# A sixth Strassen group, tanh gates and a deeper attention pipeline in a hybrid encoder layer

## The chip, the cores and the metric

The kernel runs on one core of one Trainium2 chip. The metric is the device time of one execution, in microseconds, as the median over runs. The engines are named as in the profile: PE (TensorE, the matrix engine; PEld is its loading of weights), DVE (VectorE), ACT (ScalarE), POOL (GpSimd) and SP (SyncE, which here only issues transfers).

## The reference

One encoder layer over 1024 tokens of width 1024, in float32: half a SwiGLU step, a mixer with two attention branches and gates, half a SwiGLU step, and a final norm.

```python
h = x + 0.5 * swiglu(rms_norm(x, ffn1_norm), ...)            # D_FF = 2816
u = rms_norm(h, mix_norm)
qa, ka, va, qb, kb, vb, ga, gb = split(u @ w_in)             # 512 x 4, 128, 128, 1024, 1024 columns
ya = neighbourhood_attention_2d(qa, ka, va, rpb)             # 8 heads of 64, 16 x 64 grid, 8 x 16 windows
yb = windowed_gqa_sink(rope(qb), rope(kb), vb, sink)         # 8 query heads, 2 key heads, |i - j| <= 128
merged = sigmoid(ga) * (ya @ w_branch_a) + sigmoid(gb) * (yb @ w_branch_b)
h = h + merged @ w_out
h = h + 0.5 * swiglu(rms_norm(h, ffn2_norm), ...)
y = rms_norm(h, final_norm)
```

## The kernel before, in words

Every float32 operand is split into a high and a low part (`split`, lines 91 to 94: ACT copies the high part, DVE or another engine subtracts it to get the low part). Every large product is three matmuls per block of 128 x 128 weights and 512 columns: high by high, high by low, low by high (`mm3`, lines 142 to 149). There are eight PSUM banks in two tags of four, "d" and "g" (`bank`).

The large products use Strassen's scheme in Winograd's form: seven products of quarters instead of eight. For the input projection (`products`, `store_z`) the 34 column chunks of 128 are handled in groups of four chunks, two pairs each; one group is 7 products x 2 pairs x 4 blocks x 3 matmuls. The list `groups` holds five groups: all 18 chunks of queries, keys and values and the first two gate chunks (18 and 19). Chunk 18 + dc is gate chunk dc; dc 0 to 7 belong to branch A and 8 to 15 to branch B. The results go through DRAM tensors (`zs_d`, `z_d`, `g_d`) and are read back where needed.

The remaining 14 gate chunks are computed as ordinary products (`gate`: eight steps of six matmuls each, yielded one by one), and these steps are the *filler* of the attention loop. The filler goes on with branch B's output product (`branch_b`: eight chunks of four steps, each followed by the multiplication by the gate) and with the first steps of branch A's (`branch_a`). `nfill` is the number of steps, 14 x 8 + 38 = 150.

The attention loop goes over 64 units, 32 of branch B and then 32 of branch A. A unit is two heads for 128 queries. Its stages are three functions: `scores` (four matmuls into two "d" banks, on DVE the minimum with the bias, `tensor_tensor_reduce` at line 1283, on ACT the exponential, then the reciprocal on DVE and the scaling of one head's row on DVE, line 1290, and of the other on ACT, line 1291); `turn` (transposes on PE into two "d" banks, line 1299, and a split on ACT and DVE into `ws`); and `values` (matmuls into a "g" bank, lines 1313 and 1318, and the unit's `write` of its output, lines 1231 to 1259). In round n of the loop the program runs `scores` of unit n, half of the round's filler, `turn` of unit n - 1, the other half of the filler and `values` of unit n - 2. `rate`, (150 - 44) / 64 = 1.656, is the number of filler steps per round, and three steps are given in advance. What filler is left runs behind the loop. `prep_a` loads the operands of the next pair of branch A's heads on POOL's queue during the loop, lines 1090 and 1092, and transposes its values, line 1104. Instructions are put in order by a scheduler that follows the order of the program and may move ready ones ahead; the waits follow from what each instruction reads and writes.

Branch B's attention output is collected in an `xs` tile and written to `y_d` from POOL's queue once in four units; branch A's in `fa[:, 3072:4096]`, once in four units, with the last pair of heads split into slots 22 and 23 behind the loop. The rows of the softmax lie in `fa` from column 1536 on, in two pairs used in turn. Behind the loop come branch A's output product with its gates (`a_prep`, `combine`), the product with `w_out` (`Down` with a scale of 1.0), and the second SwiGLU.

## Time and profile before

| | us |
|---|---|
| median of 3 runs | 1935.5 |
| lowest and highest run | 1934.52 and 1937.35 |
| profiled execution: span from the first to the last instruction | 1934.8 |
| of it: attention loop, about | 283 (842 to 1125) |
| of it: input projection behind the norm, about | 197 (645 to 842) |

The profile gives the profiled execution's time only as its span; what lies around the span is not in it, and the median of the runs stands 0.7 us above the span. The mean granted clock of PE is 0.998 of full speed.

How to read it: the page gives the busy time of each engine, their shares in 40 slices, and the chain of work that ended last. The groups of instructions give, behind the shapes and the count, the busy time in us and the mean duration of one in ns, and behind the next bar the idle time of the engine just before them and what ended it. The order of time gives start, duration, engine, line and operation. A stretch's row gives the busy time of PE, PEld, DVE, ACT and POOL (with the number of instructions), then the granted clock, the share of the DMA engines and GB/s.

### The profile page before, as it was taken

Reading aid. Unit: us, or ns where it says so; the run is one execution under the profiler, and the core shown is the slowest. Engines: PE = TensorE matmul, PEld = TensorE weight load, DVE = VectorE, ACT = ScalarE, POOL = GpSimd, SP = SyncE. Lnnn points to the kernel's source line nnn. Section 1 sums busy time; section 2 is a strip of 40 time slices with the busy share of each in tenths; the row PEclk is TensorE's granted clock in tenths of the full one; section 3 lists DMA queues with packets and bytes.
Section 4 is the critical chain, followed back from the end, with each engine's and each line's share of the span. In section 5 each row is a group of like instructions: output and inputs, shape, how many; then the busy total and the mean of one; then the engine's idle time right before and its main releaser. Section 6 shows DMA issues by size and latency. Waiting matters only on the chain.

```text
span 1934.8 us, 25499 instructions
## 1 busy us (share of the span) xinstructions
PE 1922.2 (99%) x8956; PEld 1603.1 (83%) x8956; DVE 1437.1 (74%) x2560; ACT 943.6 (49%) x1827; POOL 295.5 (15%) x432
## 2 busy tenths in 40 slices
PE   9999999999999999999999999999999999999998
PEld 7888888888888888888888888878888888888886
DVE  7987765668957788678888857889676566569864
ACT  6532333344446543477877862365333333344453
POOL 0011110013300112211122231010111001005210
PEclk9999999999999999999999999999999999999999
DMA  6344323286234478553458576533423323493341
GB/s 261 100 167 163 129 104 128 86 289 225 88 109 137 159 223 250 185 163 104 116 134 195 184 242 210 169 140 133 147 87 109 126 87 109 140 355 104 112 144 61
DMA packets 151745, 298.70 MB, mean 154 GB/s; under 512 B 14912, under 2 KB 64448, under 8 KB 151616
## 3 DMA queue, kind: packets, MB, share of 16 engines
q1 hardware_dynamic: 123072, 210.53, 33.6%
q0 software_dynamic: 27824, 85.48, 13.3%
q8 instruction: 71, 1.16, 0.3%
q10 hardware_dynamic: 720, 1.05, 0.1%
q14 instruction: 58, 0.48, 0.1%
HBM read 210.50 MB, written 88.27 MB: 154 GB/s over the span
## 4 chain that ended last, share of the span: by engine, by line
PE 88%; issue 7%; POOL 1%; DMA 1%; DVE 1%; ACT 1%; POOLq 0%; SPq 0%; ACTq 0%; DVEq 0%
PE g L149 16%; PE g L147 16%; PE g L145 16%; PE d L149 11%; PE d L147 11%; PE d L145 11%; PE d L1299 2%; PE g L1313 1%; PE g L1318 1%; PE d L1278 1%; PE d L1279 1%; POOL zs_d L889 1%; PE d L138 1%; POOL z_d L891 1%; DMA zr_d<-xs 0%
## 5 line engine op out<-in xcount | busy, mean ns | idle before, releaser
L145 PE MATMUL g<-ar,ws 128*128 128x512 f32 x1128 | 423.1, 395 | 0.6 <-ACT fa L911 0.6
L147 PE MATMUL g<-ar,ws 128*128 128x512 f32 x1128 | 417.2, 390 | 0.9 <-DVE ar L94 0.5
L149 PE MATMUL g<-ar,ws 128*128 128x512 f32 x1128 | 416.1, 390 | 0.2 <-DVE ws L311 0.2
L145 PE MATMUL d<-ar,ws 128*128 128x512 f32 x736 | 282.4, 391 | 0.3 <-ACT ar L810 0.2
L147 PE MATMUL d<-ar,ws 128*128 128x512 f32 x736 | 281.9, 390 | 0.3 <-DVE ar L812 0.3
L149 PE MATMUL d<-ar,ws 128*128 128x512 f32 x736 | 281.6, 390 | 0.5 <-DVE ws L311 0.5
L147 PEld LDWEIGHTS g<-ar,ws 128*128 128x128 f32 x1128 | 211.8, 188 | 46.2 <-DVE ar L94 1.0
L149 PEld LDWEIGHTS g<-ar,ws 128*128 128x128 f32 x1128 | 211.7, 188 | 45.5 <-DVE ws L311 0.7
L145 PEld LDWEIGHTS g<-ar,ws 128*128 128x128 f32 x1128 | 206.4, 188 | 37.8 <-ACT fa L911 1.0
L311 DVE TENSOR_TENSOR ws<-raw,ws 128x512 fp32r<-128x512 f32 x204 | 139.6, 690 | 99.6 <-ACT ws L308 98.8
L308 ACT CAST ws<-raw 128x512 fp32r<-128x512 f32 x204 | 125.1, 620 | 140.6 <-PE g L149 64.4
L145 PEld LDWEIGHTS d<-ar,ws 128*128 128x128 f32 x736 | 138.3, 188 | 29.7 <-ACT ar L810 0.6
L147 PEld LDWEIGHTS d<-ar,ws 128*128 128x128 f32 x736 | 138.4, 188 | 29.6 <-DVE ar L812 0.6
L149 PEld LDWEIGHTS d<-ar,ws 128*128 128x128 f32 x736 | 138.4, 188 | 29.4 <-DVE ws L311 0.7
L93 ACT CAST ws<-raw 128x512 fp32r<-128x512 f32 (+1 forms) x121 | 81.0, 669 | 144.0 <-PE d L149 61.8
L94 DVE TENSOR_TENSOR ws<-raw,ws 128x512 fp32r<-128x512 f32 (+1 forms) x119 | 93.7, 789 | 59.8 <-ACT ws L93 59.3
L414 POOL DMA_DIRECT2D hid<-fx x91 | 49.3, 542 | 431.5 <-DVE fx L474 304.9
L93 ACT CAST ar<-raw 128x512 fp32r<-128x512 f32 (+1 forms) x83 | 56.0, 679 | 94.8 <-PE g L147 55.0
L94 DVE TENSOR_TENSOR ws<-ar,ws 128x512 fp32r<-128x512 f32 x114 | 98.3, 867 | 3.8 <-ACT ws L93 3.7
L145 PE MATMUL g<-ws,ws 128*128 128x512 f32 x232 | 91.0, 392 | 0.0
L149 PE MATMUL g<-ws,ws 128*128 128x512 f32 x232 | 90.5, 390 | 0.0
L147 PE MATMUL g<-ws,ws 128*128 128x512 f32 x232 | 90.3, 389 | 0.0
(313 smaller groups left out, 3607.4 us busy)
## 6 DMA issues: line engine op xcount, KB each, us to landing
raw<-hid SPq DMA_DIRECT2D x70, 512.0 KB
hid<-fx POOLq DMA_DIRECT2D x91, 256.0 KB, 2.4
ar<-in_ffn_w_down_dram SPq DMA_DIRECT2D x32, 512.0 KB
raw<-in_ffn_w_up_dram SPq DMA_DIRECT2D x31, 512.0 KB
raw<-in_ffn_w_gate_dram SPq DMA_DIRECT2D x27, 512.0 KB
raw<-in_w_in_dram SPq DMA_DIRECT2D x27, 512.0 KB
hid<-fa POOLq DMA_DIRECT2D x51, 256.0 KB, 2.7
ar<-zs_d POOLq DMA_DIRECT2D x48, 256.0 KB, 5.3
```

The costliest lines, as they stand in the source:

```text
L93: nc.scalar.copy(dst_hi, src)
L94: (eng or nc.vector).tensor_tensor(dst_lo, src, f32v(dst_hi), op=ALU.subtract)
L138: nc.tensor.transpose(pt[:, c * P:(c + 1) * P], xs[:, (half * 4 + c) * P:(half * 4 + c + 1) * P], ident)
L145: nc.tensor.matmul(b, lhs[0], r[0], start=first, stop=False, **kw)
L147: nc.tensor.matmul(b, lhs[0], r[1], start=False, stop=False, **kw)
L149: nc.tensor.matmul(b, lhs[1], r[0], start=False, stop=last, **kw)
L308: nc.scalar.copy(w[0][:, :512], a)
L311: nc.vector.tensor_tensor(w[0][:, 512:], a, f32v(w[0][:, :512]), op=ALU.subtract)
L414: nc.gpsimd.dma_start(hid[PRODUCTS.index(p), i], src)
L889: nc.gpsimd.dma_start(d[ch * P:(ch + 1) * P, cols], t)
L891: nc.gpsimd.dma_start(z_d[ch * P:(ch + 1) * P, cols], c)
L1299: nc.tensor.transpose(pt[:, i * P:(i + 1) * P], un["pr"][s][:, i * P:(i + 1) * P], ident)
```

## The change

- `groups` gets a sixth group, gate chunks 20 to 23 (dc 2 to 5). Ten gate chunks are left for the filler, and `nfill` becomes 118.
- The gates' sigmoid becomes tanh: sigmoid(x) = (1 + tanh(x / 2)) / 2. ACT computes tanh(x / 2), DVE computes (tanh + 1) times the branch's product in one instruction, and the factor of one half goes into the scale of the product with `w_out`.
- In the loop, `turn` works on unit n - 2 and `values` on unit n - 3. The rows of the softmax get a third pair in `fa`, and the small statistics a third buffer. `rate` becomes (118 - 17) / 67 = 1.507.
- GpSimd takes over the copy of the sink logit (before on DVE), the scaling of the second head's row (before on ACT), and the low parts of the filler's gate weights and of branch B's weights (before on DVE).
- The attention output is added up in one DVE instruction of 64 partitions in place of two, in `hs` tiles, and written to `y_d` from SP's queue in place of POOL's, once in two units; the transfer puts the halves into their rows. The last pair of heads is split within the loop, once in four units.
- Branch B's gates are fetched two chunks ahead, in halves, into `xs` or `hs` tiles, and opened one chunk ahead.

```diff
-    groups = [[(12, 13), (14, 15)], [(16, 17), (0, 1)], [(4, 5), (8, 9)], [(2, 3), (6, 7)], [(10, 11), (18, 19)]]
+    groups = [..., [(10, 11), (18, 19)], [(20, 21), (22, 23)]]
...
+    def fetch_gate(dc):
+        r = xs4() if dc % 3 < 2 else None
+        rb = [hs4() if r is None else r[:, n * 512:(n + 1) * 512] for n in range(2)]
+        for n in range(2):
+            nc.sync.dma_start(rb[n], g_d[D + dc * P:D + (dc + 1) * P, n * 512:(n + 1) * 512])
         return rb
+    def open_gate(rb):
+        for r in rb:
+            nc.scalar.activation(r, r, AF.Tanh, scale=0.5)
...
-        nxt = branch_w(wb[0], 0, nc.vector), gate_b(0)
+        w, rbs = branch_w(wb[0], 0, nc.gpsimd), [fetch_gate(dc) for dc in range(2)]
+        open_gate(rbs[0])
         for dc in range(NC8):
             bs = [bank("dg"[dc % 2]) for _ in range(2)]
-            yield from branch_mm(bs, w, Y_B)
-            if dc + 1 < NC8:
-                nxt = branch_w(wb[0], dc + 1, nc.vector), gate_b(dc + 1)
+            mm = branch_mm(bs, w, Y_B)
+            for c in range(4):
+                drain(mm, 1)
+                yield
+                if c == 0 and dc + 2 < NC8:
+                    rbs.append(fetch_gate(dc + 2))
+                if c == 1 and dc + 1 < NC8:
+                    nxt = branch_w(wb[0], dc + 1, nc.gpsimd)
+                    open_gate(rbs[dc + 1])
+            w = nxt
             for n in range(2):
-                nc.vector.tensor_tensor(merged(dc)[:, sl], bs[n], rb[:, sl], op=ALU.mult)
+                nc.vector.scalar_tensor_tensor(out=merged(dc)[:, sl], in0=rbs[dc][n], scalar=1.0, in1=bs[n],
+                                               op0=ALU.add, op1=ALU.mult)
...
-                yield from gate(dc, {4: lambda: mix.update(gate=load_w(win[0], GA + nxt * P))})
+                yield from gate(dc, {4: lambda: mix.update(gate=load_w(win[0], GA + nxt * P, eng=nc.gpsimd))})
...
-                    for s in range(2):
-                        nc.vector.tensor_tensor(ybox["b"][s * HD:s * HD + HD, c, :], o[:HD, s, :], lo[:, s, :], op=ALU.add)
-                    if c == 3:
-                        nc.gpsimd.dma_start(y_d[:512, j * P:(j + 1) * P].rearrange("(c p) t -> p c t", p=P), ybox["b"])
+                    nc.vector.tensor_tensor(ybox["b"][:, c % 2], o[:HD], lo, op=ALU.add)
+                    if c % 2:
+                        nc.sync.dma_start(y_d[(c - 1) * P:(c + 1) * P, j * P:(j + 1) * P].rearrange("(c s p) t -> p c s t", s=2, p=HD),
+                                          ybox["b"])
...
+                    if hp == 3:
+                        ...
+                        if j % n == n - 1:
+                            cols = slice((j - n + 1) * P, (j + 1) * P)
+                            split(slot(22)[:, cols], slot(23)[:, cols], ybox["a"])
+                        return
...
-            pr = fa[:, 1536 + (2 * (npair[0] % 2) + s) * (384 + ext):][:, :ext + nw]
+            pr = fa[:, 1536 + (2 * (npair[0] % 3) + s) * (384 + ext):][:, :ext + nw]
             if ext:
-                nc.vector.tensor_copy(pr[:, 0:1], un["sink"][s])
+                nc.gpsimd.tensor_copy(pr[:, 0:1], un["sink"][s])
...
-        nc.scalar.activation(un["pr"][1], un["pr"][1], AF.Copy, scale=rc[:, 1:2])
+        nc.gpsimd.tensor_scalar(un["pr"][1], un["pr"][1], rc[:, 1:2], None, op0=ALU.mult)
...
-    rate = (nfill - 44) / 64.0
+    rate = (nfill - 17) / 67.0
...
-        if len(pipe) > 1 and pipe[1] is not None:
-            turn(pipe[1])
+        if len(pipe) > 2 and pipe[2] is not None:
+            turn(pipe[2])
...
-        if len(pipe) > 2 and pipe[2] is not None:
-            values(pipe[2])
-        pipe = pipe[:3]
+        if len(pipe) > 3 and pipe[3] is not None:
+            values(pipe[3])
+        pipe = pipe[:4]
...
-    split(slot(22), slot(23), fa[:, 3072:4096])
...
-    down = Down(4, wo[0], 1.0, place, quarter, ...
+    down = Down(4, wo[0], 0.5, place, quarter, ...
...
-        nc.scalar.activation(r, r, AF.Sigmoid)
+        nc.scalar.activation(r, r, AF.Tanh, scale=0.5)
...
-            nc.vector.tensor_tensor(r[:, sl], bs[n], r[:, sl], op=ALU.mult)
+            nc.vector.scalar_tensor_tensor(out=r[:, sl], in0=r[:, sl], scalar=1.0, in1=bs[n], op0=ALU.add, op1=ALU.mult)
```

More of the change, by code (lines that the diff above doesn't have):

```diff
@@ L872, in trunk_kernel @@
     mix = {}
-    groups = [[(12, 13), (14, 15)], [(16, 17), (0, 1)], [(4, 5), (8, 9)], [(2, 3), (6, 7)], [(10, 11), (18, 19)]]
+    groups = [[(12, 13), (14, 15)], [(16, 17), (0, 1)], [(4, 5), (8, 9)], [(2, 3), (6, 7)], [(10, 11), (18, 19)], [(20, 21), (22, 23)]]
     NG = len(groups)
@@ L1174, in merged, with hs4 @@
         return slot((16, 17, 18, 19, 24, 25, 26, 27)[dc])
-    def gate_b(dc):
-        rb = xs4()
-        nc.sync.dma_start(rb, g_d[D + dc * P:D + (dc + 1) * P, :])
-        nc.scalar.activation(rb, rb, AF.Sigmoid)
-        return rb
+    def hs4():
+        return main.tile([P, 512], F32, tag="hs", bufs=6, name=nm_("hs"))
+    def fetch_gate(dc):
[3 more added lines that the diff above has]
+            nc.sync.dma_start(rb[n], g_d[D + dc * P:D + (dc + 1) * P, n * 512:(n + 1) * 512])
+        return rb
+    def open_gate(rb):
+        for r in rb:
+            nc.scalar.activation(r, r, AF.Tanh, scale=0.5)
     def branch_b():
@@ L1248, in write @@
                 def write(o, j=j, hp=hp):
-                    y = fa[:, 3072:4096]
+                    n = 4 if hp == 3 else 2
+                    if j % n == 0:
+                        ybox["a"] = hs4()
                     lo = mix["lo"][:HD, j % 2]
@@ L1386, in trunk_kernel @@
     loads[0].append(lambda d: d.load_left(2))
-    down = Down(4, wo[0], 1.0, place, quarter, {k: left_d[i] for i, k in enumerate(("P5", "P6", "P3", "P7"))},
+    down = Down(4, wo[0], 0.5, place, quarter, {k: left_d[i] for i, k in enumerate(("P5", "P6", "P3", "P7"))},
                 loads, (8, 10))
```

21 lines of the change are left out of this document (11 added, 10 removed).

## The prediction, made before the change was run

> **What bounds the kernel now.** I read the page first, then the order of time of the matrix engine (PE), then the busy time by stretch, then the groups of instructions inside the attention loop.
>
> ```profile
> span 1934.8 us, 25499 instructions
> PE 1922.2 (99%) x8956; PEld 1603.1 (83%) x8956; DVE 1437.1 (74%) x2560; ACT 943.6 (49%) x1827; POOL 295.5 (15%) x432
> PE 88%; issue 7%; POOL 1%; DMA 1%; DVE 1%; ACT 1%; POOLq 0%; SPq 0%; ACTq 0%; DVEq 0%
> ```
>
> PE is busy 99% and carries 88% of the chain that ended last. But PE ends are modelled, so I look at starts. In the projection (order of time, PE only):
>
> ```profile
> 700.03 0.39 PE L145 MATMUL d<-ar,ws 128*128 128x512 f32 x1
> ...
> 705.93 0.39 PE L149 MATMUL g<-ar,ws 128*128 128x512 f32 x1
> ```
>
> These two stand 26 matmuls apart: 5.90 / 26 = 0.227 us per 128x512 matmul; the 0.39 is latency, not cost. Now the busy time by stretch: projection, attention of branch B, attention of branch A (two rows), and what follows the loop.
>
> ```profile
> 645.00:842.00 197.00, 196.31 (x881) 162.12 (x880) 155.72 (x234) 95.37 (x169) 34.27 (x64) 1.00 0.68 207
> 842.00:982.00 140.00, 139.34 (x817) 121.95 (x815) 114.79 (x392) 110.39 (x280) 21.02 (x36) 1.00 0.46 127
> 982.00:1046.00 64.00, 63.99 (x386) 56.55 (x385) 55.98 (x178) 51.99 (x139) 11.62 (x22) 1.00 0.64 153
> 1046.00:1125.00 79.00, 79.00 (x468) 69.32 (x467) 66.95 (x211) 66.75 (x164) 23.35 (x25) 1.00 0.68 188
> 1125.00:1175.00 50.00, 50.00 (x222) 41.11 (x221) 19.42 (x30) 24.23 (x31) 12.35 (x10) 1.00 0.77 253
> ```
>
> The columns are PE, weight loads, DVE, ACT, POOL, clock, DMA. PE has no gap to win back: 0.7 us idle in the projection, 0.7 us in the loop, clock 1.00. So the time falls only by fewer matmuls and rises by whatever PE comes to wait for. DVE and ACT have their least room in the loop (82 to 87%, and 79 to 84%); POOL stands at 15 to 30%.
>
> **Part 1, the sixth Strassen group.** Gate chunks 2 to 5 leave the filler: 4 chunks x 8 blocks x 6 matmuls = 192. A group adds 7 products x 2 x 4 blocks x 3 = 168. Net 24 fewer, 24 x 0.227 = **-5.4 us**. The group's splits, combinations and POOL stores lie in a stretch with DVE at 155.72 / 197 = 79% and ACT at 48%, beside continuous PE, and stores and next loads follow the pattern of the five groups there: 0 us. If that cover were gone, the nearest price is that stretch's present loss, 0.7 us.
>
> **Part 2, the loop with less filler.** A filler step is 6 matmuls. Before, 150 steps, of which 3 + 67 x 1.656 = 114 run in the loop and 36 behind it; after, 118, of which 3 + 68 x 1.507 = 105.5 in the loop and 12.5 behind. So the loop's cover per unit shrinks, and branch B's output product (32 steps, from step 81, near unit 52) now runs inside. One unit in the PE's order of time:
>
> ```profile
> 903.40 0.34 PE L1278 MATMUL d<-ar,ar 128*128 128x384 f32 x1
> ...
> 904.11 0.63 PE L145 MATMUL g<-ar,ws 128*128 128x512 f32 x2
> ...
> 905.50 0.82 PE L1299 MATMUL d<-ident,fa 128*128 128x128 f32 x6
> 906.07 0.96 PE L1318 MATMUL g<-ws,fx 128*128 128x256 f32 x6
> 906.87 0.34 PE L1278 MATMUL d<-ar,ar 128*128 128x384 f32 x1
> ```
>
> Scores 0.71, one step 1.39, transposes 0.57, values 0.80. The loop took the 140 + 64 + 79 = 283 us of its three rows for 67 rounds, 4.22 each; 0.149 steps less make 4.22 - 0.21 = 4.02 us. What the other engines must fit into that:
>
> ```profile
> L1291 ACT ACTIVATE fa<-fa,rc 128x384 f32<-128x384 f32 x48 | 29.9, 623 | 1.5 <-DVE rc L1289 1.4
> L1282 DVE COPY fa<-nsk 128x1 f32<-128x1 f32 x64 | 8.5, 142 | 4.6 <-DMA z_d<-fa 3.8 <-ACT fa L1286 0.5 <-DMA g_d<-fa 0.3
> L1233 DVE TENSOR_TENSOR xs<-g,s 64x128 f32<-64x128 f32 x64 | 18.0, 281 | 1.0 <-ACT s L1231 0.2
> L1253 DVE TENSOR_TENSOR s<-g,s 64x256 f32<-64x256 f32 x32 | 13.2, 411 | 2.6 <-ACT s L1252 2.3
> L94 DVE TENSOR_TENSOR ws<-raw,ws 128x1024 fp32r<-128x1024 f32 x13 | 15.9, 1224 | 3.4 <-ACT ws L93 3.2
> L94 POOL TENSOR_TENSOR ar<-raw,ar 128x1024 fp32r<-128x1024 f32 x6 | 14.8, 2464 | 22.0 <-ACT ar L93 22.0
> L126 POOL TENSOR_SCALAR st<-st 128x1 f32<-128x1 f32 x20 | 7.6, 379 | 206.3 <-ACT xs L123 206.0
> L1197 DVE TENSOR_TENSOR ar<-d,xs 128x512 f32<-128x512 f32 x8 | 5.2, 686 | 9.6 <-PE d L149 8.3 <-ACT xs L1179 1.1
> L913 DVE SCALAR_TENSOR_TENSOR fa<-d,fa 128x512 f32<-128x512 f32 x16 | 10.9, 686 | 4.0 <-PE d L149 3.8
> L1179 ACT ACTIVATE xs<-xs 128x1024 f32<-128x1024 f32 x8 | 8.5, 1061 | 10.8 <-DMA xs<-g_d 10.7
> ```
>
> DVE per round: branch B 114.79 / 140 x 4.22 = 3.46, less two sink copies 0.28, less the second write 2 x 0.28 - 0.41 = 0.15, less the gate weights' low part 1.22 x 1.656 / 8 = 0.25, gives 2.8 of 4.02 (69%). Branch A 66.95 / 79 x 4.22 = 3.58, less 0.15 and 0.25, 3.2 (79%). Where branch B's product runs beside it, two gate products per four steps add 2 x 0.69 x 1.507 / 4 = 0.52: 3.7 (92%). The scalar-tensor-tensor that replaces L1197 costs what L1197 does: L913 runs it on one input from PSUM and one from SBUF in the same 0.69.
>
> ACT: branch B 3.33 less the scaling 0.62 is 2.7 (67%); branch A 3.57 - 0.62 = 2.95 (73%); beside the product, four steps bring 512 columns of weights and 1024 of tanh, 1.5 x 1.06 = 1.6 (up to 1.9 in halves), for half a gate's split and copies, 1.06: at most 0.3 a round, 3.2 (80%).
>
> POOL: two sink copies (0.38 each at most), the scaling of 384 columns, and a gate's low part 2.46 x 1.507 / 8 = 0.46. The scaling has no row: below lies 0.38 (one column), above the two-input rate, 2.46 x 384 / 1024 = 0.92. It has one input, so I take 0.7, between them. With the 0.6 it has now, 2.5 of 4.02 at most. No engine passes PE: 0 us.
>
> **Part 3, latency.** The softmax of a unit must be done when its transposes come up.
>
> ```profile
> 903.96 0.62 DVE L1283 CUSTOM_DVE_ANT_0 fa<-d,masks,nsk 128x384 f32<-128x384 f32 x1 [0.50 <-PE d L1279]
> 905.11 0.62 DVE L1283 CUSTOM_DVE_ANT_0 fa<-d,masks,nsk 128x384 f32<-128x384 f32 x1
> 906.88 0.62 ACT L1291 ACTIVATE fa<-fa,rc 128x384 f32<-128x384 f32 x1
> 908.96 0.82 PE L1299 MATMUL d<-ident,fa 128*128 128x128 f32 x6
> ```
>
> The unit started at 903.40, was scaled by 907.50, and was transposed from 908.96: 1.46 us spare. One unit deeper gives 4.02 more, the slower scaling takes 0.1 to 0.3 back: about 5.2 us spare. On POOL a queued gate split (2.46) fits into that; so do the sink copies, which can run once the unit three before has been transposed. POOL's queue also holds prep_a's loads, which wait for PE:
>
> ```profile
> POOL ar L1092 <- PE d L1279: 17.2, 3, 12.2
> ```
>
> If scalings stand behind the longest of these, 12.2 - 5.2 = 7 us are lost once (1937); I take 0, since units in hand come ahead of prep_a in the program. On SP, the writes of y now wait for DVE ahead of later weight loads; those are asked for four steps, 4 x 1.39 us, and the units between them, ahead: 0 us.
>
> **Part 4, around the loop.** Behind it PE keeps 12.5 steps, 17 us, where there were 49; the row 1125 to 1175 shows DVE 39% and ACT 48% busy there, half of it branch B's product that has moved into the loop. 0 us. At the loop's start PE waits once, behind DVE (chain, in order of time):
>
> ```profile
> 848.67 1.24 DVE ar L94
> ...
> 849.95 0.50 PE g L147
> ```
>
> Nothing in the change moves that split's place, so I leave its wait; if the freed DVE removes it, about 1.2 us more are won.
>
> **Sum.** 1934.8 is the span; the median of the runs, 1935.5, stands 0.7 above it, and I leave that as it is. 1935.5 - 5.4 = **1930.1 us**, 0.28% less. About 0.2% (3.9 us) is what a measurement of this kernel can tell from no change.
>
> **Rivals.**
>
> *GpSimd and DVE get in each other's way.* In the trace, by source line:
>
> ```profile
> L94 DVE TENSOR_TENSOR ws<-ar,ws x114: 676/685/1793, 421.3 to 1901.7; 128x512 fp32r<-128x512 f32 x114
> L94 DVE TENSOR_TENSOR ws<-d,ws x128: 411/550/560, 852.4 to 1121.2; 128x384 fp32r<-128x384 f32 x96, 128x256 fp32r<-128x256 f32 x32
> L1290 DVE TENSOR_SCALAR fa<-fa,rc x64: 336/420/966, 850.0 to 1117.7; 128x384 f32<-128x384 f32 x48, 128x256 f32<-128x256 f32 x16
> ```
>
> A DVE subtraction with both inputs in SBUF takes up to 1.79 instead of 0.69, the scaling L1290 once 0.97, while the subtraction from PSUM never passes 0.56. The Trainium skill ("SBUF — State Buffer", Who interferes with whom) says why and speaks against this change: DVE and GpSimd share a port pair, taken whole by a DVE instruction with two SBUF inputs or in a two-port mode, or by GpSimd's. The rows agree with it. By that rule each move to GpSimd costs DVE something too. Here the loop's DVE work is mostly from PSUM, and what is exposed is L1290 once a unit: 0.97 - 0.34 = 0.6. In the units beside the product (15 rounds) DVE goes to 3.7 + 0.6 = 4.3 against 4.02, so 0.3 x 15 = 4 us, and with the last head pair's splits (1.1 each, 4 of them) 8 us: 1934 to 1938. Against it: it needs POOL to be ahead at nearly every unit. Chance 0.22.
>
> *PSUM banks, slower than before.* Even chunks of branch B's product take two of the four "d" banks for four steps, 2.65 rounds, and now do so while scores and transposes need them: chunks 0, 2 and 4, about 8 rounds. With two banks left, scores wait for the low parts of the transposes before them and transposes wait for the scores' minimum:
>
> ```profile
> 900.64 0.82 PE L1299 MATMUL d<-ident,fa 128*128 128x128 f32 x6
> ...
> 902.91 0.56 DVE L94 TENSOR_TENSOR ws<-d,ws 128x384 fp32r<-128x384 f32 x1 [0.16 <-ACT ws L93]
> ```
>
> From scores to the second minimum 905.73 - 903.40 = 2.33, from transposes to the last low part 903.47 - 900.64 = 2.83: 5.16 in a row, and 0.5 for the gate products (2 x 0.69 per 2.65 rounds). If nothing overlaps, (5.66 - 4.02) x 8 = 13 us: 1943. If halves overlap as they do now (0.35 at each hand-over) and filler is put between, near 0. It ends slower than before from 5.4 us of waits, and measurably from 9.3 us, 1.2 a round. For it: DVE at 92% exactly there. Against it: prep_a's own transposes (L1104) take "d" banks today, and the waits of PE's weight loads show 0.3 us for them in the whole loop:
>
> ```profile
> PEld d L1104 <- DVE ws L94: 0.3, 1, 0.3
> ```
>
> Chance 0.15, two thirds of it measurably slower.
>
> *The activation table.* Sigmoid cost a load after the loop's exponentials:
>
> ```profile
> 1130.45 1.28 ACT L1179 ACT_TABLE_LOAD   x1
> ```
>
> If tanh needs another table than exp, six chunks x 2 x 1.28 = 15.4 us fall on ACT inside the loop: 3.2 x 16 + 15.4 = 66.6 against 64.3 available, 2 us at least, 15 at most: 1932 to 1945. The Trainium skill ("ScalarE: Activation LUTs", Table sets: the hidden batching unit) lists tanh in the set of exp, by which this costs nothing; the trace before cannot show it. Chance 0.04, nearly all of it slower.
>
> *The count doesn't fall* (the group runs and PE loses as much between its products): 1935.5. Chance 0.02.
>
> **How the numbers follow.** PE stays fed: 0.57, with its own range from 1928.6 (the start's 1.2 and prep_a's 0.3 gone) to 1931.6 (1.5 us of new waits), all of it faster. Same: 0.21 of the port, 0.05 of the banks, 0.02 of the count, 0.28. Slower: 0.01 of the port above its sum, 0.10 of the banks, 0.04 of the table, 0.15. The range runs from 1928.6 less half the runs' spread (1934.52 to 1937.35, so 1.4), 1927.2, to 1939.0, which leaves the slower cases out.
>
> **What would show it.** Right: 24 fewer 128x512 matmuls, starts 0.227 apart, the projection about 38 us longer, rounds near 4.0 us, no PE wait of over 1 us in the loop, one table load for it. Wrong: PE waiting on "d" tiles from unit 52 on (banks), L1290 near 0.97 in the median (port), table loads among the tanh, or transposes waiting on POOL.

## The result, and the profile after

The changed kernel takes 1948.27 us (median of 5 runs, 1945.26 to 1951.55) beside 1936.05 us of the kernel before in the same comparison (5 runs, 1934.52 to 1938.03): a ratio of 1.0062, 95% interval 1.0052 to 1.0073. It is slower by 12 us, where 5.4 us less were predicted. Its profiled execution took 1947.41 us, 2.1 us more than its span. The 0.7 us that the prediction found before the change set a median beside the span of another execution; in the comparisons below, an execution of the kernel before takes 1.7 to 1.9 us more than its own span. A trace shows one execution, and executions of one kernel differ along with the clock that PE was granted: of the changed kernel's five, the one with a span of 1943.3 us has a mean clock of 0.997, the one with 1949.5 us has 0.993.

The page of the changed kernel: span, busy time, PE's granted clock in 40 slices, and the engines' shares of the chain that ended last.

```profile
span 1945.3 us, 25733 instructions
PE 1921.5 (99%) x8932; PEld 1601.0 (82%) x8932; DVE 1429.5 (73%) x2448; ACT 915.4 (47%) x1781; POOL 413.0 (21%) x567
PEclk9999999999999999999999899999999999999999
PE 86%; issue 6%; DMA 2%; ACT 2%; DVE 2%; POOL 2%; SPq 0%; POOLq 0%; ACTq 0%; DVEq 0%
```

24 matmuls are gone, as counted, yet PE's busy time fell by 0.7 us only, and one slice of the clock fell below full: something between 1070 and 1120 us both stopped PE and slowed it. To see which units, I take the first score matmul of units 0, 48 and 63 in PE's order of time, before (L1278) and after (L1303):

```profile
841.93 0.28 PE L1278 MATMUL d<-ar,ar 128*128 128x256 f32 x1
1049.99 0.28 PE L1278 MATMUL d<-ar 128*128 128x256 f32 x1
1114.61 0.28 PE L1278 MATMUL d<-ar,ar 128*128 128x256 f32 x1
```

```profile
879.02 0.28 PE L1303 MATMUL d<-ar,ar 128*128 128x256 f32 x1
1077.17 0.28 PE L1303 MATMUL d<-ar 128*128 128x256 f32 x1
1154.08 0.38 PE L1303 MATMUL d<-ar,ar 128*128 128x256 f32 x1
```

| stretch | before, us | after, us | difference |
| --- | --- | --- | --- |
| up to the loop | 841.9 | 879.0 | +37.1 |
| units 0 to 48 | 208.1 (4.33 a unit) | 198.2 (4.13) | -9.9 |
| units 48 to 63 | 64.6 (4.31) | 76.9 (5.13) | +12.3 |
| from there to the end | 820.2 | 791.2 | -29.0 |

Nearly all of the loss is in the last 15 units, in which branch B's output product now runs. At the 4.13 us of the first 48 they would take 62.0, which is 14.9 less, and the span would end at 1930.4; the forecast, put on the span, is 1929.4. The stretches of the changed kernel by busy time (PE, weight loads, DVE, ACT, POOL, clock, DMA share, GB/s): the projection, the two parts of the loop, and the 24 us in which it happens.

```profile
683.00:879.00 196.00, 195.50 (x866) 161.60 (x865) 138.44 (x203) 82.27 (x142) 33.04 (x63) 1.00 0.64 195
879.00:1077.00 198.00, 195.86 (x1168) 172.98 (x1167) 154.49 (x461) 140.33 (x373) 121.09 (x168) 1.00 0.51 138
1077.00:1154.00 77.00, 67.39 (x370) 57.22 (x369) 61.03 (x172) 53.76 (x135) 44.74 (x37) 0.89 0.67 188
1086.00:1110.00 24.00, 14.94 (x60) 11.95 (x58) 14.56 (x31) 12.18 (x30) 13.76 (x12) 0.64 0.84 220
```

In these 24 us PE is busy for 14.94 at a mean clock of 0.64. A narrower row shows the clock at half of full speed for 17 us:

```profile
1092.50:1109.50 17.00, 10.15 (x32) 8.13 (x33) 8.75 (x23) 8.11 (x18) 7.26 (x6) 0.50 0.69 214
```

PE's order of time shows four waits, each with what ended it:

```profile
1089.66 0.62 PE L149 MATMUL g<-ar,ws 128*128 128x512 f32 x2
1093.63 1.54 PE L1324 MATMUL d<-ident,fa 128*128 128x128 f32 x6 [3.34 <-DVE ws L94]
...
1097.27 1.95 PE L1338 MATMUL g<-ws,fx 128*128 128x256 f32 x6 [0.39 <-DVE ws L94]
1103.44 1.22 PE L145 MATMUL d<-ar,ws 128*128 128x512 f32 x2 [4.22 <-ACT ws L93]
1104.46 1.05 PE L147 MATMUL d<-ar,ws 128*128 128x512 f32 x2
1106.63 1.22 PE L149 MATMUL d<-ar,ws 128*128 128x512 f32 x2 [1.11 <-POOL ws L94]
```

What DVE and POOL did before the first of them:

```profile
1088.57 4.67 DVE L1315 TENSOR_SCALAR fa<-fa,rc 128x384 f32<-128x384 f32 x1
```

```profile
1088.27 4.75 POOL L94 TENSOR_TENSOR ar<-raw,ar 128x1024 fp32r<-128x1024 f32 x2
```

Y_B[0] to Y_B[3] are the four blocks of rows of branch B's attention output, read back for its output product. The row scaling L1315 takes 0.42 us in the median. This one began while POOL subtracted to get the low parts of Y_B[0] and Y_B[1], and ended with them. Everything on DVE stood behind it, the low parts for the transposes first. The last two waits are for branch B's first weights. SP's queue and the chain in order of time show how these come late:

```profile
1095.07 0.58 SPq L1283 DMA_DIRECT2D y_d<-hs  x1
...
1096.86 0.32 SPq L1153 DMA_DIRECT2D raw<-y_d  x1
1097.27 0.93 SPq L1131 DMA_DIRECT2D raw<-in_w_branch_b_dram  x2
```

```profile
1096.86 4.95 DMA raw<-y_d
...
1102.96 2.39 POOL ar L94
1105.34 1.24 POOL ws L94
...
1106.63 1.22 PE d L149 x2
```

A write of y waits for the held DVE; behind it on SP stand the fetch of a gate and that of Y_B[3], and behind them the weights. ACT's cast and POOL's subtraction of Y_B[3] then stand ahead of those of the weights.

### The profile page after: what moved, and what is told of

The parts are those of the page before. It is cut to its first block, busy times and chain, and to the rows that moved or that the text cites. A ratio compares the mean times of both kernels' runs of the same rounds, so it can differ in the third digit from the quotient of the medians.

```text
span 1945.3 us, 25733 instructions
## 1 busy us (share of the span) xinstructions
PE 1921.5 (99%) x8932; PEld 1601.0 (82%) x8932; DVE 1429.5 (73%) x2448; ACT 915.4 (47%) x1781; POOL 413.0 (21%) x567
## 3 DMA queue, kind: packets, MB, share of 16 engines
q10 hardware_dynamic: 720, 1.05, 0.1%
## 4 chain that ended last, share of the span: by engine, by line
PE 86%; issue 6%; DMA 2%; ACT 2%; DVE 2%; POOL 2%; SPq 0%; POOLq 0%; ACTq 0%; DVEq 0%
PE g L149 16%; PE g L145 16%; PE g L147 16%; PE d L149 11%; PE d L145 11%; PE d L147 11%; PE d L1324 2%; PE g L1343 1%; PE d L1303 1%; PE d L1304 1%; PE g L1338 1%; ACT fa L1311 1%; PE d L138 1%; POOL zs_d L889 1%; POOL z_d L891 0%
## 5 line engine op out<-in xcount | busy, mean ns | idle before, releaser
L145 PE MATMUL g<-ar,ws 128*128 128x512 f32 x1096 | 413.6, 394 | 0.5 <-ACT fa L911 0.5
L147 PE MATMUL g<-ar,ws 128*128 128x512 f32 x1096 | 409.5, 390 | 0.4 <-DVE ar L833 0.4
L149 PE MATMUL g<-ar,ws 128*128 128x512 f32 x1096 | 408.8, 390 | 0.2 <-DVE ws L311 0.2
L145 PE MATMUL d<-ar,ws 128*128 128x512 f32 x760 | 293.0, 392 | 4.6 <-ACT ws L93 4.2
L149 PE MATMUL d<-ar,ws 128*128 128x512 f32 x760 | 291.5, 390 | 1.6 <-POOL ws L94 1.1
L147 PE MATMUL d<-ar,ws 128*128 128x512 f32 x760 | 292.2, 390 | 0.3 <-DVE ar L812 0.3
L149 PEld LDWEIGHTS g<-ar,ws 128*128 128x128 f32 x1096 | 205.6, 188 | 44.2 <-DVE ws L311 0.7
L147 PEld LDWEIGHTS g<-ar,ws 128*128 128x128 f32 x1096 | 205.7, 188 | 43.8 <-DVE ar L833 0.8
L145 PEld LDWEIGHTS g<-ar,ws 128*128 128x128 f32 x1096 | 201.2, 188 | 37.3 <-ACT fa L911 0.9
L311 DVE TENSOR_TENSOR ws<-raw,ws 128x512 fp32r<-128x512 f32 x210 | 143.6, 689 | 107.8 <-ACT ws L308 106.9
L145 PEld LDWEIGHTS d<-ar,ws 128*128 128x128 f32 x760 | 142.7, 188 | 34.5 <-ACT ws L93 4.5
L149 PEld LDWEIGHTS d<-ar,ws 128*128 128x128 f32 x760 | 142.7, 188 | 31.8 <-POOL ws L94 1.8
L147 PEld LDWEIGHTS d<-ar,ws 128*128 128x128 f32 x760 | 142.8, 188 | 30.1 <-DVE ar L812 0.9
L93 ACT CAST ws<-raw 128x512 fp32r<-128x512 f32 (+1 forms) x117 | 76.5, 656 | 140.2 <-PE d L149 61.3
L94 DVE TENSOR_TENSOR ws<-raw,ws 128x512 fp32r<-128x512 f32 x98 | 71.5, 730 | 53.2 <-ACT ws L93 53.2
L1316 POOL TENSOR_SCALAR fa<-fa,rc 128x384 f32<-128x384 f32 (+1 forms) x64 | 82.0, 1282 | 61.9 <-DVE rc L1314 40.7
L1311 ACT ACTIVATE fa<-fa,nmx 128x385 f32<-128x385 f32 (+3 forms) x128 | 75.6, 591 | 41.5 <-DVE nmx L1308 38.4
L145 PE MATMUL g<-ws,ws 128*128 128x512 f32 x232 | 91.0, 392 | 0.0
```

The source lines that it names most:

```text
L93: nc.scalar.copy(dst_hi, src)
L94: (eng or nc.vector).tensor_tensor(dst_lo, src, f32v(dst_hi), op=ALU.subtract)
L145: nc.tensor.matmul(b, lhs[0], r[0], start=first, stop=False, **kw)
L147: nc.tensor.matmul(b, lhs[0], r[1], start=False, stop=False, **kw)
L149: nc.tensor.matmul(b, lhs[1], r[0], start=False, stop=last, **kw)
L311: nc.vector.tensor_tensor(w[0][:, 512:], a, f32v(w[0][:, :512]), op=ALU.subtract)
```

## The experiments

Two theories at first: that POOL's long subtractions hold DVE (the expectations call it A, or the port), and B, the weights' load chain at branch B's head. A third, C, is that the loop's filler cover, the PE work that runs while a unit passes the other engines, is too thin. The head of branch B's product is the place where it begins. Later theories are named where they come in: banks (the product takes PSUM banks from the units), load (it brings DVE and ACT too much work) and burst (its head and the preparation of the last head pair fall together). The time of each is its median and the ratio to the kernel before of its own comparison, which lay between 1935.2 and 1936.3 us.

**Y_B's low parts on DVE.**

```diff
-split_y(Y_B[c], c * P, nc.gpsimd) for c in range(2)
+split_y(Y_B[c], c * P, nc.vector) for c in range(2)
-split_y(Y_B[c], c * P, nc.vector if c == 2 else nc.gpsimd)
+split_y(Y_B[c], c * P, nc.vector)
```

> The changed kernel with one thing undone: the low parts of branch B's attention output (four subtractions of 1024 columns, two of them back to back on GpSimd at 1088 us) are made on DVE. Theory A (port): these two subtractions hold what DVE's scaling L1315 needs (4.67 us in place of 0.42), the transposes and the write of y come late, and all that follows is late because of that. A expects L1315 to stay under 1.5 us, the wait of 3.5 us gone, the later waits mostly gone, 1948 to about 1935. Theory B (late start): the wait from 1097 to 1107 is of its own, since branch B's first weights and outputs are fetched behind writes of y on SP's queue and split behind each other on ACT and GpSimd. B expects 3 to 5 us won only: 1943 to 1945, with PE still waiting 6 us or more for the first weights.

Measured: 1942.2 us, 1.0035 (1.0025 to 1.0046): 6.1 of the 12 us are gone by the medians, about half of what theory A forecast. They need not be the hold's alone: POOL's work on Y_B[3] also stood ahead of that on the first weights, and the edit takes both away. The last 15 units, and the same 24 us:

```profile
1077.00:1147.00 70.00, 63.84 (x369) 53.26 (x367) 62.47 (x173) 53.06 (x134) 37.38 (x33) 1.00 0.73 210
1086.00:1110.00 24.00, 20.38 (x118) 16.56 (x117) 20.48 (x55) 18.44 (x46) 10.76 (x12) 1.00 0.86 227
```

No wait is longer than 1.5 us, and the clock stays at 1.00. (The trace is of an execution of 1939.43 us, 2.8 below the median.) But the units still take 4.68 us, not 4.13, and DVE is now busy for 89% of them. Nor is the hold gone. DVE's own subtraction of a row of Y_B, usually 1.21 us, takes 2.69 beside POOL's for the first weights:

```profile
1094.14 2.69 DVE L94 TENSOR_TENSOR ar<-raw,ar 128x1024 fp32r<-128x1024 f32 x1
```

```profile
1094.44 1.30 POOL L94 TENSOR_TENSOR ws<-raw,ws 128x512 fp32r<-128x512 f32 x1
```

**The first head's scaling on ACT.**

```diff
-nc.vector.tensor_scalar_mul(un["pr"][0], un["pr"][0], rc[:, 0:1])
+nc.scalar.activation(un["pr"][0], un["pr"][0], AF.Copy, scale=rc[:, 0:1])
```

> The changed kernel, but the first head's row is scaled on ACT in place of DVE (the second stays on GpSimd), so that DVE has no single-input scaling in SBUF left. Theory A: with nothing on DVE for GpSimd's pair of subtractions to hold, the 3.5 us wait goes and most of the later ones: about 1935 to 1938, if ACT (0.62 more in each unit) keeps up. Theory B: the first weights are as late as before, 1943 to 1945. A third reading, that it is GpSimd's own lateness (its scaling takes 1.39) that PE waits for: no gain, 1948.

Measured: 1948.05, 1.006 (1.0045 to 1.0075), the number of the third reading, GpSimd's own lateness. But the trace shows a hold again: with the scaling gone from DVE, POOL's pair held another instruction:

```profile
1092.80 3.73 DVE L94 TENSOR_TENSOR ar<-raw,ar 128x1024 fp32r<-128x1024 f32 x1
```

```profile
1090.66 4.78 POOL L94 TENSOR_TENSOR ar<-raw,ar 128x1024 fp32r<-128x1024 f32 x2
```

That is DVE's own part of Y_B, usually 1.21 us. The hold belongs to POOL's instructions, not to the scaling. (Against the third reading stands the run further down in which POOL's scaling is left out.)

**A lower filler rate, so that branch B's product begins behind the loop.**

```diff
-rate = (nfill - 17) / 67.0
+rate = (nfill - 44) / 64.0
```

> The changed kernel with one number changed, the filler rate of the kernel before, (118 - 44) / 64 = 1.156 in place of 1.507, so that branch B's output product begins behind the loop and a round has 3.7 us of PE work in place of 4.0. Theories A and B both put the loss where that product begins inside the loop, and expect it gone: 1931 to 1934. If other parts (GpSimd's scaling, the deeper pipeline, less cover for each unit) cost something through the whole loop, it stays above 1938 with waits spread over the units.

Measured: 1944.27, 1.0041 (1.0027 to 1.0055), where A and B expected 1931 to 1934. The long stops are gone: no wait of PE in the last 15 units is longer than 2.0 us, and the clock stays at 1.00. But the loop pays for the thin cover. PE's own need would be 4.13 - (1.507 - 1.156) x 1.39 = 3.64 us a unit; it took 3.71 in the first 48 and 3.87 in the last 15, 7 us in all.

**The writes of y on POOL's queue.**

```diff
-nc.sync.dma_start(y_d[(c - 1) * P:...
+nc.gpsimd.dma_start(y_d[(c - 1) * P:...
-nc.sync.dma_start(y_d[512 + hp * P:...
+nc.gpsimd.dma_start(y_d[512 + hp * P:...
```

> The changed kernel with the writes of y back on GpSimd's queue, so that SP's later fetches stand behind no write that waits for DVE. Theory B: branch B's first weights and outputs are fetched earlier and the wait from 1097 to 1107 shrinks by 5 us or more: 1940 to 1943. Theory A: L1315 is held as long as before and the first wait stays; the fetches behind it come only as much earlier as SP stood still, 0 to 3 us: 1945 to 1949.

Measured: 1946.51, 1.0058 (1.0038 to 1.0079). By the medians SP's order ahead of the weights is worth 1.8 us, which the runs (1945.1 to 1952.5) don't separate from nothing.

**The kernel before, with the group alone.**

```diff
-... [(2, 3), (6, 7)], [(10, 11), (18, 19)]]
+... [(2, 3), (6, 7)], [(10, 11), (18, 19)], [(20, 21), (22, 23)]]
```

> The kernel before with the sixth Strassen group alone: four gate chunks as filler, branch B's product behind the loop as before, so 74 filler steps on 64 units (1.16 a unit, before 1.66); pipeline, sigmoid and engines untouched. Theory C (the loop needs its cover: with fewer filler steps a unit it waits for DVE and ACT, and the prediction's Part 1 is not kept): the 24 matmuls of 0.227 us are saved (5.4 us), and small PE waits of together 5 to 15 us appear all along the loop: 1935 to 1945. Theories A and B (the loss belongs to branch B's product inside the loop alone: GpSimd's long subtractions, and the load chain at its head) expect no new wait: 1935.6 - 5.4 = 1930.

Measured: 1944.21, 1.0047 (1.003 to 1.0064), within theory C's range. Its units take 3.81 and 4.02 us at 1.16 steps, against 3.64 that PE needs: 14 us. The count is saved and more than spent in the loop. Set beside the run of the changed kernel at 1.16 steps (3.71 and 3.87), the deeper pipeline, the tanh and the use of POOL save 7 us in these units. Of that the whole profiled executions show 2.4 (1944.38 and 1942.0) and the medians nothing (1944.21 and 1944.27).

**The changed kernel without the group.**

```diff
-... [(10, 11), (18, 19)], [(20, 21), (22, 23)]]
+... [(10, 11), (18, 19)]]
```

> The changed kernel without the sixth group: five groups, fourteen... that is four chunks more of gate filler, all else as changed (branch B's product still begins inside the loop, with 1.99 filler steps a unit where the changed kernel has 1.51 and the kernel before 1.66). 24 matmuls (5.4 us) come back. Theories A and B (the two waits of 3.6 and 6 to 9 us come with branch B's head, whatever the cover): the same two PE waits at the place where branch B's product begins, 1948.3 + 5.4 = 1953, or 1945 to 1950 if the thicker cover takes up part. Theory C (cover): the waits shrink to almost nothing, 1935 to 1938.

Measured: 1945.91, 1.0055 (1.004 to 1.007). With the fullest cover of all, 4.78 us in the first 48 units, the last 15 take 5.41: 9.5 us lost. PE's waits there:

```profile
PE d L149 <- POOL ws L94: 3.1, 1, 3.1
PE d L1303 <- DVE ar L1212: 2.4, 1, 2.4
```

So what the change does in the loop costs some 10 us by itself, and cover does not hide it. Each half of the change costs by itself nearly what both cost together (9.0 and 10.7 us of 12.2), as if each used up a reserve that the other needs; that reading is not tested further.

**Branch B's first weights fetched and split early.**

```diff
+7: lambda: mix.update(w0=branch_w(wb[0], 0, nc.gpsimd, mix['w0']))
-5: lambda: [fetch_y(c * P) for c in range(2, 4)]
+5: lambda: [mix.update(w0=fetch_branch(raw4()[:, :512], wb[0], 0))] + [fetch_y(...) for c in range(2, 4)]
-w, rbs = branch_w(wb[0], 0, nc.gpsimd), [...]
+w, rbs = mix.pop('w0'), [...]
```

> The changed kernel with branch B's first weights fetched ahead of the rows of Y_B[2] and Y_B[3] and split behind the last gate chunk, ahead of both; nothing else moves. Theory B (PE's second wait, 4.2 + 1.1 us for the weights, is the load chain: a transfer behind Y_B[3]'s on SyncE's queue, and the casts and subtractions in order behind it): the wait for the weights goes, and with it the stretch at half clock; the first wait (3.5 us on the held row scaling) stays: 1939 to 1943. Theory A (GpSimd's long subtractions delay all of it; the chain follows from them): the wait moves to another tile of the same moment (Y_B[2], Y_B[3]) and the time stays at 1946 to 1949.

Measured: 1946.06, 1.0054 (1.0039 to 1.0069). The wait of 4.2 us for the first weights is gone, and the clock is halved for 3.4 us in place of 17. The wait behind the held scaling is still 3.34 us, and new ones of 1.4, 1.3 and 1.1 us stand behind it, the last for the second chunk's weights. By the medians 2.2 us of time went, which the intervals don't separate from nothing; the last 15 units take 4.99 for 5.13. Theory B's chain was there, but what it cost came back in other waits: it isn't the cause by itself.

**Both of these.** (The edits of the first and of the last run.)

> Both edits: the low parts of the rows of Y_B on DVE instead of GpSimd (alone: 1942.2), and branch B's first weights fetched and split ahead of Y_B[2] and Y_B[3]. Theories A and B together (two causes): both waits at branch B's head are gone, and what is left over the kernel before is the small waits of a thinner loop (3 to 5 us) against the 5.4 us that the group saves: 1933 to 1938. If the waits in the loop outside branch B's head count more (theory C): 1939 to 1942, no better than with the first edit alone.

Measured: 1944.73, 1.0045 (1.003 to 1.006), runs from 1941.5 to 1946.2: not better than the first edit alone.

**All of branch B's products in the "g" banks** (with Y_B on DVE, as in the next three).

```diff
-bs = [bank("dg"[dc % 2]) for _ in range(2)]
+bs = [bank("g") for _ in range(2)]
```

> The changed kernel with Y_B's low parts on DVE (alone: 1942.2, 6.6 us above the kernel before) and, new, all of branch B's products in the four "g" banks, so that no chunk takes two of the "d" banks from scores and transposes. Banks theory (the prediction's second rival): PE's waits for "d" tiles from unit 50 on (scores and transposes that wait for DVE's low parts of the transposes before) go: 1937 to 1939, the rounds 48 to 63 go from 4.7 to about 4.3 us. Load theory (branch B's product brings more DVE and ACT work into rounds in which DVE stands at 87%; what comes late isn't made up, and the waits move to whatever tile is next): 1941 to 1944, the waits on other lines.

Measured: 1943.36, 1.0039 (1.0024 to 1.0054). The banks by themselves are not it.

**A rate between.**

```diff
-rate = (nfill - 17) / 67.0
+rate = 1.35
```

> The changed kernel with Y_B's low parts on DVE and the filler rate at 1.35 steps a unit in place of 1.51: branch B's product begins near unit 57 instead of 51, so a third of it is in the loop instead of two thirds, and the rounds ahead of it fall from 4.13 to about 3.9 us. Load theory: less of branch B's work in the loop means less waiting there, and 3.9 us is still above the 3.75 us at which the loop ran with 1.16 steps: 1936 to 1940. Cover theory (any thinner cover loses more than it saves): 1943 to 1946. Banks theory: fewer chunks in the loop's "d" banks, 1939 to 1941.

Measured: 1947.32, 1.0061 (1.0044 to 1.0077), the wrong way for the load theory: 3.96 us in the first 48 units, where PE needs 3.91, and 4.67 in the last 15. It pays for both.

**Branch B's tanh at the gate's copy.**

```diff
-nc.scalar.copy(gt[:, n * 512:(n + 1) * 512], bs[n])
+nc.scalar.activation(gt[:, n * 512:(n + 1) * 512], bs[n], AF.Tanh, scale=0.5)   # dc >= 8
-open_gate(rbs[0])
-open_gate(rbs[dc + 1])
```

> The changed kernel with Y_B's low parts on DVE and the tanh of branch B's gates taken where ACT copies a gate chunk out of PSUM (the copy becomes the tanh), so that the sixteen tanh of 0.64 us at branch B's product, which wait in ACT's order for the gates' transfers, are gone. Load theory: 10 us of ACT's work less in 14 rounds, and ACT's order no longer waits for a transfer; ACT stands at 80% there: 1938 to 1941. Banks theory, and DVE's share of the load theory: no change, 1941 to 1943.

Measured: 1942.25, 1.0033 (1.002 to 1.0046). 10 us of ACT's work gone, and nothing of the time.

**Y_B on DVE, "g" banks and early tanh.**

> Three edits: Y_B's low parts on DVE, branch B's products all in the "g" banks, its gates' tanh taken early. If banks and ACT's load both hold: 1934 to 1938. If only one of them does: as that one alone. If neither does (DVE's load, or the order of all of it): 1941 to 1944.

Measured: 1940.45, 1.0021 (1.0012 to 1.003), the best of all, and still slower than before; the 1.8 us below the first edit alone are not clear of the spread. The last 15 units take 4.50.

**Less work on DVE, and on POOL.** Y_B on DVE, and one scaling of each unit left out:

```diff
-nc.vector.tensor_scalar_mul(un["pr"][0], un["pr"][0], rc[:, 0:1])
```

> The changed kernel with Y_B's low parts on DVE (alone: 1942.2), with the row scaling of the first head of each unit left out (L1315, DVE 0.42 us a unit; the output is not normalised there). Load theory (DVE at 87 to 95% in the rounds beside branch B's product): DVE gets 10% of a round back and PE's waits there fall to a third or less: 1934 to 1937. If GpSimd's slow scaling or the order of the queues is the cause: 1940 to 1943.

```diff
-nc.gpsimd.tensor_scalar(un["pr"][1], un["pr"][1], rc[:, 1:2], None, op0=ALU.mult)
```

> The changed kernel with Y_B's low parts on DVE (alone: 1942.2), with the row scaling of the second head of each unit left out (L1316, GpSimd 1.39 us a unit; the output is not normalised there). If GpSimd's scaling is the cause (its 1.39 us in the softmax's latency, its queue of scalings behind the splits, or the time in which it holds DVE): 1934 to 1937. Load theory of DVE: DVE's work stays, no more than the stretched instructions fall: 1940 to 1943.

Measured: 1941.17, 1.0032 (1.0021 to 1.0042), and 1943.09, 1.0036 (1.0024 to 1.0047). Neither 10% less work on DVE nor a POOL without its scaling moves these units much. What held the first one's head, from the waits of all engines between 1085 and 1130 us:

```profile
DVE ws L94 <- ACT ws L93: 4.6, 5, 2.2
ACT ar L93 <- DMA raw<-y_d: 3.3, 2, 2.0
PE g L1337 <- DVE ws L94: 2.7, 1, 2.7
```

I read them together: ACT's cast of a row of Y_B waits for its transfer with the casts of the unit behind it; DVE waits for ACT, and PE for DVE.

**POOL's subtractions in pieces** (on the changed kernel).

```diff
-split(h, l, r, eng)
+nc.scalar.copy(h, r)
+for a in range(0, 8, 2):
+    c = slice(a, a + 2) if r0 < 512 else slice(a * P, (a + 2) * P)
+    eng.tensor_tensor(l[:, c], r[:, c], f32v(h[:, c]), op=ALU.subtract)
```

> The changed kernel with every low part of the 1024-column rows (Y_B and Y_A) in four pieces of 256 columns, on the engines that have them in the changed kernel. If a GpSimd subtraction holds DVE until it ends and lets it in between two instructions: a DVE instruction is held for one piece, 0.6 us, and not for 4.7; the first PE wait (3.5 us) goes: 1941 to 1944. If DVE does not get in between GpSimd's instructions that stand ready one behind the other: the scaling is held for 4 us or more as before, 1946 to 1949.

Measured: 1949.6, 1.0071 (1.0054 to 1.0088). DVE does not get in between the pieces:

```profile
1088.13 5.52 DVE L1318 TENSOR_SCALAR fa<-fa,rc 128x384 f32<-128x384 f32 x1
```

```profile
1088.44 5.78 POOL L1165 TENSOR_TENSOR ar<-raw,ar 128x256 fp32r<-128x256 f32 x8
```

Eight pieces of 0.72 us that stand ready one behind the other hold DVE as one instruction would.

**Is it a burst?** The last head pair prepared three units later; the product's head ahead of that pair; everything spread (each with Y_B on DVE):

```diff
-preps = {0: 23, 1: 33, 2: 41, 3: 49}
+preps = {0: 23, 1: 33, 2: 41, 3: 52}
```

> The changed kernel with Y_B's low parts on DVE (alone: 1942.2), with the last head pair's preparation begun at unit 52 instead of 49, behind branch B's head instead of beside it (eight casts on ACT and eight low parts on DVE of 0.4 us each leave those rounds). Burst theory: the waits at units 48 to 53 halve: 1937 to 1940; some of them may return at units 55 to 57, where the pair is due. Otherwise 1941 to 1944.

```diff
-rate = (nfill - 17) / 67.0
+rate = 1.66
```

> The changed kernel with Y_B's low parts on DVE and 1.66 filler steps a unit, the rate of the kernel before: branch B's head comes at unit 47, ahead of the last head pair's preparation, and the rounds up to there have the cover they had before (4.3 us). Burst theory: 1937 to 1941, few waits up to unit 56; at the end of the loop, where the filler runs out, at most 4 us of waits. Theory that branch B's product brings its waits wherever it stands in the loop: 1941 to 1945.

```diff
+preps 3: 52, early weights, "g" banks and early tanh as above
-4: lambda: [split_y(Y_B[c], c * P, nc.vector) for c in range(2)]
+3: lambda: split_y(Y_B[0], 0, nc.vector)
+4: lambda: split_y(Y_B[1], P, nc.vector)
+if dc == 0 and c == 2: split_y(Y_B[3], 3 * P, nc.vector)   # was at the head
```

> All that the runs so far point to: Y_B's low parts on DVE, branch B's products in the "g" banks, its gates' tanh taken early (these three: 1940.5), and new: the last head pair's preparation at unit 52, the four splits of Y_B one to a filler step instead of two and two, branch B's first weights ahead of its last two rows. Burst theory: 1932 to 1936, faster than or level with the kernel before. Otherwise 1939 to 1942.

Measured: 1942.94, 1.0039 (1.0026 to 1.0052); 1947.65, 1.0063 (1.0046 to 1.0079); 1941.55, 1.0027 (1.0018 to 1.0036). The burst theory's gain came with neither of the first two. With the pair later, waits of 1.95 and 1.57 us stay at the product's head. With the head earlier, the waits at the head itself are small (0.82, 0.17 and 0.38 us), but 13 us behind it PE waits for 2.53 us. That wait leads back to the product too: ACT stood for 4.84 us before the tanh of a gate whose transfer had not landed, with the next unit's exponentials behind it. In the last run the chain of the head has yet another link:

```profile
1093.65 1.24 POOL fa L1320
1094.89 1.26 POOL ws L94
...
1096.19 0.73 PE g L149 x2
```

Here the weights' low part stands in POOL's order behind a scaling. Its last 15 units take 4.50:

```profile
1078.00:1146.00 68.00, 62.63 (x370) 53.46 (x369) 62.26 (x172) 46.62 (x121) 38.48 (x33) 1.00 0.76 216
```

PE and DVE are each busy for 92% of them.

## Why the prediction was wrong, point by point

**Part 1 held.** 168 matmuls more ahead of the loop are 168 x 0.227 = 38.1 us; the loop starts 37.1 later. In the row 683 to 879 PE idles for 0.5 us. The rival "the count doesn't fall" is out. The wait that the prediction left at the loop's start is gone; PE had lost 0.53 us by it, not 1.2. In the first 48 units PE now waits twice, at 894.94 and 962.45, for a copy on ACT:

```profile
PE g L1343 <- ACT xs L1127: 2.1, 2, 1.5
```

**Part 2 held for 48 units, with one size off.** Predicted were rounds 0.21 us shorter; 4.33 - 4.13 = 0.20 were measured. (The prediction's 4.22 and 4.02 spread the loop over 67 rounds.) DVE stood at 78%, ACT at 71%. POOL's scaling was priced at 0.7 us between 0.38 and 0.92, and lies outside both ends:

```profile
L1316 POOL TENSOR_SCALAR fa<-fa,rc x64: 912/1386/1589, 885.8 to 1159.2; 128x384 f32<-128x384 f32 x48, 128x256 f32<-128x256 f32 x16
```

1.39 us at 384 columns, 3.6 ns a column (1.24 us, 3.2 ns, in the run with the first head's scaling on ACT), where the subtraction with two inputs takes 2.38 / 1024 = 2.3 ns. The bound was wrong because it held one input to be cheaper than two. It didn't decide: without that scaling the kernel gained nothing.

**Part 3 failed at "a queued gate split (2.46) fits into that".** The step weighed POOL's queue against the 5.2 us in which one unit's softmax may be late. But POOL's subtraction doesn't only delay the work behind it on POOL: it held DVE, whose order carries several units at once. And the subtractions that did it are Y_B's, for which the prediction's POOL sum has no term of its own. With Y_B's off POOL 6.1 us of time went by the medians, PE's first wait of 3.3 us among them. The change did not put Y_B's low parts on POOL; it moved them beside other units. Before it, the same pair ran in the loop's last rounds, and the scaling that came up 1.6 us into it was held only until the first of the two ended:

```profile
1116.09 4.82 POOL L94 TENSOR_TENSOR ar<-raw,ar 128x1024 fp32r<-128x1024 f32 x2 [7.05 <-ACT ar L93]
```

```profile
1117.69 0.97 DVE L1290 TENSOR_SCALAR fa<-fa,rc 128x256 f32<-128x256 f32 x1
```

Why DVE got in between the two there and not after the change stays open. The step's other zero, SP's, held for the later weights ("asked for four steps ahead"), but the first weights are asked for at the head itself.

**Part 4 failed at "half of it branch B's product that has moved into the loop. 0 us".** This is the step that turned the sign. Work that had been under PE's cover behind the loop, with DVE at 39% and ACT at 48%, moved to units whose engines were at 70 to 80% and whose order is fixed. The last 15 units lost 15 us by the first 48's pace; PE's four waits there make 3.34 + 0.39 + 4.22 + 1.11 = 9.1. In the 17 us at half clock PE worked for 10.15, an estimated 5.1 more than at full clock. Together these are 14.2 of the 15.

**Why an average of 92% didn't warn.** Part 2 added up busy time and found each engine under 4.02 us. The runs show that busy time isn't the limit: 0.42 us less of DVE a unit gained 1 us in all, within the spread, and 10 us less of ACT nothing. Each unit's work passes PE, ACT, DVE and PE again in fixed orders, and one transfer, cast or hold that comes late is met by three other engines. By which wait it shows depends on the version: DVE's hold, the weights' load, Y_B's transfer, POOL's order. About 6 us of the 12 are shown to come with Y_B's low parts on POOL, by its hold of DVE and by its order together. Of the rest it is shown that it sits at branch B's product inside the loop, for it is there with more cover and with an earlier head, and that none of banks, tanh, DVE's or POOL's scaling, the first weights or the head pair removes it alone. No run took all of POOL's subtractions off it, so its hold may have a part in the rest too. Which chain would have to be shortened is left open.

**The rivals.** *GpSimd and DVE* was right in its mechanism and wrong in its place: the prediction expected it at L1290 once a unit, at 0.97, and 1934 to 1938. L1315 stands at 0.42 in the median. Five of the 64 took over 1 us (1.06 twice, 1.99, 2.16 and 4.67), and only the longest is followed by a stop of PE:

```profile
L1315 DVE TENSOR_SCALAR fa<-fa,rc x64: 352/422/4671, 885.0 to 1159.1; 128x384 f32<-128x384 f32 x48, 128x256 f32<-128x256 f32 x16
```

The Trainium skill ("SBUF — State Buffer", Who interferes with whom) says that whoever issues first has the shared pair for the whole instruction and the other blocks. The changed kernel's trace agrees in that POOL's pair began first, at 1088.27, and DVE's scaling at 1088.57. It goes further, since the hold lasted over two instructions, and over eight (5.52 us). Two traces differ: in pieces, the held scaling began at 1088.13, 0.31 us ahead of POOL's first, and with Y_B on DVE, the stretched subtraction began 0.30 us ahead of POOL's. So the order of the recorded starts doesn't decide here who is held. *PSUM banks*: its sign was there (PE waited for "d" tiles, 3.3 and 4.2 us), but with every product in "g" the time stayed at 1943.4 for 1942.2; a wait on a bank's tile was a wait for who fills or drains it. *The activation table* is out: one load at the loop's start, none until the next stage.

```profile
880.82 1.28 ACT L1311 ACT_TABLE_LOAD   x1
```

```profile
1319.12 1.28 ACT L470 ACT_TABLE_LOAD   x1
```

The last also dates the loss: before the change this load came at 1308.63, 10.5 us earlier, and the spans differ by 10.5.

## What to carry to other kernels

When work moves from a stretch with idle engines into a loop that runs near the limit of several, don't price it by busy time: follow one unit through the engines' orders and ask what stands behind each transfer, cast and wait that is added. GpSimd instructions with long SBUF operands that stand ready in a row can act as one hold of DVE, so put them where no DVE instruction on SBUF is urgent; cutting them into pieces did not help here. And a saving in one stage is only kept if the next stage didn't live on the work that was moved.

## What the runs showed of the hardware

A GpSimd queue of two-input subtractions held a DVE scaling of 0.42 us for 4.67 us (two of 1024 columns) or 5.52 us (eight of 256), and a DVE subtraction of 1.21 us for 3.73. It did not always hold over the whole queue: before the change the scaling beside such a pair took 0.97. DVE's subtraction from PSUM never passed 0.56 us in the rows of the kernel before. GpSimd's scaling by a column of factors takes 3.2 to 3.6 ns a column, more than its two-input subtraction (2.3).

A wait of PE can cost more than its length: the clock fell to 0.50 within the wait of 3.34 us, the six transposes behind it took 1.54 us for the usual 0.82, and two matmuls of 512 columns 1.05 for 0.63, until 1109.5 us. The Trainium skill ("TensorE: Matmul & The Clock Gate", What's actually happening) puts the window after which an idle PE drops to half its clock, and the busy one after which it returns, at about 3.4 us. The lengths agree: in the traces of this case that show a halved clock in the loop, it lasts 3.4, 6.8, 10.2, 13.7 or 17.1 us, whole steps of 3.41. That a single wait must be so long does not show: at the rate between, the clock fell behind a wait of 2.28 us, and without the group it stayed at 1.00 behind one of 3.06. With Y_B on DVE, where no wait passed 1.5 us, it stayed at 1.00.
